# Moving the products with v and the pool differences in a fused decoder layer

## The chip, the cores and the metric

One core of a Trainium2 chip runs the whole layer in one launch. The engines used are TensorE (PE, with its weight loads PEld), VectorE (DVE), ScalarE (ACT), GpSimd (POOL) and the DMA queues that SyncE (SP), GpSimd and ScalarE fill. The metric is device time of one execution in microseconds (us), the median of the runs shown.

## What is computed

The layer takes x (512 tokens by 1024 channels, float32). One projection gives q, k, v, the input p of a pool branch and the gate logits g. The part that matters here is this, cut from the reference:

```python
q, k, v, p, g = jnp.split(proj, [ATTN_WIDTH, 2 * ATTN_WIDTH, 3 * ATTN_WIDTH, 3 * ATTN_WIDTH + POOL_WIDTH], axis=-1)
y_attn = moba_attention(q.reshape(hs), k.reshape(hs), v.reshape(hs), rel_bias) @ w_branch_attn[l]
y_pool = multiscale_pool(p, w_pool_group[l], pool_scale[l]) @ w_branch_pool[l]
...
for g, w in enumerate((2, 4, 8, 16)):                  # in multiscale_pool: 4 groups of 128 channels
    outs.append((csg[:, 1:] - lag) / cnt[None, :, None])   # mean over the last w tokens
diff = pooled - p
y = jnp.einsum('bsgc,gcd->bsgd', diff, w_group) * scale
```

Attention has 8 heads of 64 channels with a causal mask and a bias by distance. Both branches are projected, weighted by sigmoid gates, summed, projected again and normalised; a gated MLP with a causal convolution follows.

## The kernel before

Nearly every product is split: an operand a is rounded to a_hi (ACT, line 69) and the rest a_lo = a - a_hi is taken on DVE (line 70), and three matmuls hi*hi, lo*hi, hi*lo are summed in PSUM (`mm3`, lines 213, 216 and 217). Weights come in tiles of 128 x 1024 through a ring: load into `wraw`, then split into `whi` and `wlo`. `weights(i)` calls `fetch()` so that three tiles beyond the one in use have been requested (`LEAD`). The products with v (line 575) are plain float32 with a stationary operand of 64 columns, one head writing the lower and the other the upper 64 partitions of one PSUM bank.

A part of the tiles is computed in pairs with seven products in place of eight (`seven`, line 246). Each pair uses four weight tiles: A (plain), X (two loads, the second accumulating: SP at line 164, then POOL at line 165), D (SP, line 160) and Y (formed on DVE at line 175 from X and A). The matmuls of a pair write the banks named `sai`, `sbi` and `sci`. The last product of a pair, `close`, is deferred and runs when the next pair calls `flush()`. Line 267 is the final add of a pair but for that deferred product; it is kept as `state["add"]`.

In time, the part around the change runs like this. First come x and v, then pool groups 3 and 2 as plain tiles (`in_tile("p", ...)`, `PLAIN = (3, 2)`). Then the loop over n runs five pairs: n = 0 gives pool groups 0 and 1, n = 1 to 4 give two heads each (q and k tiles). Then a loop over the eight heads h does for each head: `head(h + 2)` prepares q and k, one gate tile (`in_tile`, 24 matmuls named `g`), `scores(h + 2)`, the transposes of the probabilities (`trans(h)`, line 562, copied to `PT` by ACT at 564 and DVE at 565 and 566), and for odd h `pv(h // 2)`, the products with v of both heads of a pair (16 matmuls, line 575, bank `ob`). `PT` has two buffers.

A pool group has three steps. `pool_sum` copies the projection into a padded tile and adds shifted copies (line 427), log2(w) times: four for group 3 (on DVE), three for group 2, one for group 0 and two for group 1 (on POOL). `pool_dif` forms mean minus token (lines 438 to 440, tile `dif`) and splits it into `difs`. `pool_out` makes three matmuls into bank `zb` and copies to `zT`. The tiles of sums and differences share a ring of four buffers, tag `tmp`; `difs` has two.

The order on each engine is fixed when the kernel is built. A scheduler takes the instructions traced in program order, earlier ones first where several are ready by its own model of time, and lays down one sequence for each engine and DMA queue; on the chip an instruction that waits holds everything behind it in its own sequence. `tc.issue_after(ins)` adds a constraint: what the block traces on the engine of `ins` stands behind `ins` in that engine's sequence. `AHEAD` says how many fetches early a raw tile of a pair is requested.

Of the kernel before, what the change touches and what calls it, by code (L numbers as in the profile page):

```python
# [8 lines left out]
F32 = mybir.dt.float32  # L9
F32R = mybir.dt.float32r  # L10
AF = mybir.ActivationFunctionType
ALU = mybir.AluOpType
PSUM = bass.MemoryType.PSUM

P = 128
S = 512
# [3 lines left out]
H = 8  # L20
# [10 lines left out]
PAD = 16  # L31
LEAD = 3
RING = 5
TMP = 4
PLAIN = (3, 2)
# [10 lines left out]
def layer_kernel(ctx: ExitStack, tc: tile.TileContext, xT, x, w_v, w_c, rel_bias, invcnt, w_group,  # L46
                 pscale, w_br, w_out, lnr, w_fi, convp, w_fo, out):
    nc = tc.nc
# [16 lines left out]
    def split(hi, lo, src, copy=None):  # L65
        if copy:
            copy(hi, src)
        else:
            nc.scalar.activation(hi, src, AF.Copy)  # L69
        state["lo"] = nc.vector.tensor_tensor(lo, src, hi.bitcast(F32), op=ALU.subtract)  # L70
        return state["lo"]
# [42 lines left out]
    state = {"next": 0, "limit": WO0 - 1}  # L114

    def fetch(pool=None, early=None):
        i = state["next"]
        state["next"] = i + 1
        for q, ahead in AHEAD.items():
            while coming[q]:  # L120
                key = coming[q][0]
                n, f = key
                if not homes.get((n, q)) or at[n, f, q] > i + (ahead if q != "A" or (n, f - 1) in pair_of else 0):
                    break
                fetch_raw(coming[q].pop(0), q)
        if isinstance(chunks[i], tuple):
            ready[i] = (fetch_fo if i >= FO0 else fetch_seven)(i, *chunks[i])
            return
        raw = wp.tile([P, D], F32, tag="wraw", name=f"wraw{i}", bufs=3)
        if pool is None:  # L130
            hi = wp.tile([P, D], F32R, tag="whi", name=f"whi{i}", bufs=RING)
            lo = wp.tile([P, D], F32R, tag="wlo", name=f"wlo{i}", bufs=RING)
        else:
            hi = pool.tile([P, D], F32R, name=f"whi{i}")
            lo = pool.tile([P, D], F32R, name=f"wlo{i}")
        parts = 2 if early else 1
        for c in range(parts):
            sl = slice(c * (D // parts), (c + 1) * (D // parts))
            (nc.scalar if early else nc.sync).dma_start(raw[:, sl], chunks[i][:, sl])
            split(hi[:, sl], lo[:, sl], raw[:, sl], fast if early and c == 0 else None)  # L140
            if c == 0 and early:
                early()
        ready[i] = (hi, lo)
# [10 lines left out]
    def fetch_raw(key, q):  # L154
        a, u = pair_of[key]
        r = raws[key, q] = homes[key[0], q](key[1])
        if q == "A":
            nc.sync.dma_start(r, a)
        elif q == "D":
            nc.sync.dma_start(r, u[:, S:])  # L160
        else:
            v = r.rearrange("p (a c) -> p a c", a=2)
            (pst, pn), (est, _) = u.ap
            nc.sync.dma_start(v, bass.AP(tensor=u.tensor, offset=u.offset, ap=[[pst, pn], [0, 2], [est, S]]))
            state["acc"] = nc.gpsimd.dma_start(  # L165
                v, bass.AP(tensor=a.tensor, offset=a.offset, ap=[[pst, pn], [u.offset + S - a.offset, 2], [est, S]]),
                accum_op=ALU.add)
# [58 lines left out]
    def flush():  # L226
        if pending:
            pending.pop()()
# [63 lines left out]
    pb = pooling.enter_context(tc.tile_pool(name="pb", bufs=1, side="right", reuse_waits="tile"))  # L292
# [35 lines left out]
    cinv = const.tile([P, PAD], F32, name="cinv")  # L328
# [61 lines left out]
    dif = {}  # L390
# [26 lines left out]
    def pool_sum(j, b, sign=1.0, eng=None):  # L417
        eng = eng or nc.gpsimd
        w = POOL_WINDOWS[j]
        pt = pb.tile([P, PAD + S], F32, tag="tmp", name=f"pt{j}", bufs=TMP)  # L420
        nc.gpsimd.memset(pt[:, :PAD], 0.0)
        nc.scalar.activation(pt[:, PAD:], b, AF.Copy, scale=sign)
        cur, sh = pt, 1
        while sh < w:
            nxt = pb.tile([P, PAD + S], F32, tag="tmp", name=f"pw{j}_{sh}", bufs=TMP)
            o = 2 * sh - 1
            eng.tensor_tensor(nxt[:, o:], cur[:, o:], cur[:, o - sh:PAD + S - sh], op=ALU.add)
            cur, sh = nxt, 2 * sh
        sums[j] = pt, cur

    def pool_dif(j, *behind):
        w = POOL_WINDOWS[j]
        pt, cur = sums.pop(j)
        with ExitStack() as held:
            for ins in behind:
                held.enter_context(tc.issue_after(ins.ins))
            d = pb.tile([P, S], F32, tag="tmp", name=f"dif{j}", bufs=TMP)
            nc.vector.scalar_tensor_tensor(d, cur[:, PAD:], 1.0 / w, pt[:, PAD:], op0=ALU.mult, op1=ALU.subtract)
            nc.vector.tensor_tensor(d[:, :w - 1], cur[:, PAD:PAD + w - 1], cinv[:, :w - 1], op=ALU.mult)
            nc.vector.tensor_tensor(d[:, :w - 1], d[:, :w - 1], pt[:, PAD:PAD + w - 1], op=ALU.subtract)  # L440
            dd = pb.tile([P, 2, S], F32R, tag="dif", name=f"difs{j}", bufs=2)
            dif[j] = dd[:, 0, :], dd[:, 1, :]
            split(*dif[j], d)

    def pool_out(j):
        b = bank(f"zb{j}")
        mm3(b, (wg_hi[:, j, :], wg_lo[:, j, :]), dif[j], True, True)
        nc.scalar.activation(zT[:, j, :], b, AF.Copy, scale=psc[:, j:j + 1])

    def in_tile(kind, j):  # L450
        wh, wl = split3(weights(at[kind, j]), KT)
        b = bank(f"{kind}{j}")
        for kt in range(KT):
            mm3(b, (wh[:, kt, :], wl[:, kt, :]), (xT_hi[:, kt, :], xT_lo[:, kt, :]), kt == 0, kt == KT - 1)
        if kind == "p":
            pool_sum(j, b, eng=nc.vector if j == PLAIN[0] else None)
        else:
            gslot[j] = gates[:, len(gslot), :]
            nc.vector.tensor_copy(gslot[j], b)
# [9 lines left out]
    raw_q = {}  # L469
    raw_k = {}  # L470
    in_tile("p", PLAIN[0])
    pool_dif(PLAIN[0])
    in_tile("p", PLAIN[1])

# [40 lines left out]
    for n in range(1 + pairs):  # L515
        if n == 0:
            u, done = xr[1][:, 3, :], lambda ba, u: pool_sum(0, ba)
        else:
            u = raw_k[n - 1] = av.tile([P, S], F32, tag="rk", name=f"rk{n - 1}")
            done = lambda ba, u, p=n - 1: heads_done(p, ba)  # L520
        seven(("i", n), (xT_hi, xT_lo), ti, xr[1][:, 2, n % 2 * 256:n % 2 * 256 + 256], u, done)
        if n == 0:
            pool_dif(PLAIN[1], state["add"])
            with tc.issue_after(state["acc"].ins):
                write_table(*table)
        elif n == 1:
            pool_dif(0, state["add"])
            pool_sum(1, xr[1][:, 3, :], -1.0)
            for j in PLAIN:
                pool_out(j)  # L530
        elif n == 2:
            pool_dif(1, state["add"])
            with tc.issue_after(state["acc"].ins):
                load_strip(0)
                load_strip(1)
            head(0, state["add"], state["copy"])
        elif n == 3:
            pool_out(0)
            pool_out(1)
            head(1, state["add"], state["copy"])  # L540
            pooling.close()
            aw = attn.enter_context(tc.tile_pool(name="aw", bufs=3, side="right", reuse_waits="tile"))
            scores(0)
# [25 lines left out]
    def pv(p):  # L569
        b = bank(f"ob{p}")  # L570
        for kb in range(NT):
            n = (NT - kb) * P
            for e in range(2):
                h = 2 * p + e
                nc.tensor.matmul(b[e * DH:(e + 1) * DH, kb * P:], vv[:, kb, h * DH:(h + 1) * DH],
                                 PTs[h][:, toff[kb]:toff[kb] + n], start=kb == 0, stop=kb == NT - 1)
        state["o"] = nc.scalar.activation(oT[:, p, :], b, AF.Copy)

    scores(1)
    for h in range(H):  # L580
        if h + 2 < H:
            head(h + 2, nms[h], exps[h])
        if h < H - 1:
            in_tile(*fill.pop(0))
            flush()
        if h + 2 < H:
            scores(h + 2)
        trans(h)
        if h >= 4:
            with tc.issue_after(nms[h].ins), tc.issue_after(exps[h].ins):  # L590
                split(zT_hi[:, h - 4, :], zT_lo[:, h - 4, :], zT[:, h - 4, :])
        if h == H - 1:
            in_tile(*fill.pop(0))
        if h % 2:
            pv(h // 2)
    attn.close()

    bra = ExitStack()
# [74 lines left out]
    for f in range(GSEVEN, KT):  # L673
        if f == KT - 1:
# [3 lines left out]
              lambda ba, u, f=f: gate_done(f, ba, u), first_half if f == KT - 1 else None)  # L678
# [214 lines left out]
    for f in range(last + 1, NF):  # L893
# [24 lines left out]
        for c in list(spread):  # L918
            if f >= KH + c.stop - 1 and (f > last + 1):
# [3 lines left out]
                                               op0=ALU.mult, op1=ALU.subtract)  # L923
# [167 lines left out]
```

## Time and profile before

| | before |
|---|---|
| median of 3 runs | 652.54 us (651.95 to 653.64) |
| the profiled execution | 653.2 us, of which span 651.5 us |
| instructions | 10192 |
| granted TensorE clock, mean | 0.993 |
| PE between 50 and 62 us | 8.11 us busy of 12.00 |
| PE between 66 and 80 us | 14.00 us busy of 14.00 |

Busy time is time in which an engine works on an instruction. Matmuls are pipelined, so a row's duration is longer than the step from one matmul to the next. In a row of an engine's sequence the columns are start, duration, engine, line, operation and operands; a bracket at the end gives the idle time before it and what ended it. A row of the waits is: who waited, for whom, then us in total, times and the longest.

### The profile page before, as it was taken

The page shows a single profiled execution, that of the slowest core. Times are in us where ns is not written, and L with a number is a line of the kernel's source. Part 1 is how long each engine was busy: PE and PEld are TensorE (multiplying, and loading weights), DVE is VectorE, ACT ScalarE, POOL GpSimd, SP SyncE. Part 2 cuts the span into 40 slices and gives each one's busy share as a digit, 9 for nine tenths or more (in the row PEclk, how much of TensorE's full clock was granted, in tenths as well). Part 3 has the DMA queues.
Part 4 walks back from the last instruction along what each step waited for, and adds up shares of the span by engine and source line. Part 5 has one row for each costly group of instructions (what it writes and reads, how often), then busy time and mean ns, then how long its engine had stood idle before and what let it go on. Part 6 is the DMA issues. An engine that isn't in the chain of part 4 may idle for free.

```text
span 651.5 us, 10192 instructions
## 1 busy us (share of the span) xinstructions
PE 633.7 (97%) x3910; PEld 562.6 (86%) x3910; DVE 497.3 (76%) x754; ACT 348.9 (54%) x522; POOL 115.4 (18%) x131
## 2 busy tenths in 40 slices
PE   9987999999999999999999999999999999999994
PEld 6877998777688999888998999999998888888884
DVE  6967788667477597759795788888889649798695
ACT  6634667554472555605364466566556337555452
POOL 0033305322115111210001010110101201123202
PEclk9999999999999999999999999999999999999998
DMA  8676627432158544553147767777727964889905
GB/s 315 205 165 157 160 69 244 131 97 58 58 173 213 151 111 136 177 205 103 60 149 190 174 168 194 179 196 192 179 68 274 266 201 100 207 191 198 273 1 129
DMA packets 39328, 106.11 MB, mean 163 GB/s; under 512 B 4320, under 2 KB 4584, under 8 KB 39024
## 3 DMA queue, kind: packets, MB, share of 16 engines
q1 hardware_dynamic: 26560, 71.37, 33.5%
q0 software_dynamic: 12144, 33.06, 26.0%
q10 hardware_dynamic: 576, 1.05, 0.4%
q8 instruction: 30, 0.49, 0.3%
q14 instruction: 18, 0.15, 0.1%
HBM read 100.20 MB, written 3.17 MB: 159 GB/s over the span
## 4 chain that ended last, share of the span: by engine, by line
PE 93%; DVE 3%; issue 1%; ACT 1%; POOL 1%; DMA 0%; DVEq 0%; POOLq 0%; ACTq 0%
PE fi L213 5%; PE fi L216 5%; PE fi L217 5%; PE saf L213 4%; PE saf L217 4%; PE saf L216 4%; PE v L387 3%; PE g L213 2%; PE br L213 2%; PE g L217 2%; PE wo L217 2%; PE br L216 2%; PE br L217 2%; PE wo L216 2%; PE wo L213 2%; PE g L216 2%
## 5 line engine op out<-in xcount | busy, mean ns | idle before, releaser
L70 DVE TENSOR_TENSOR wlo<-wraw,whi 128x1024 fp32r<-128x1024 f32 (+1 forms) x59 | 71.9, 1226 | 17.1 <-ACT whi L69 16.9
L69 ACT ACTIVATE whi<-wraw 128x1024 fp32r<-128x1024 f32 (+1 forms) x58 | 59.5, 1034 | 44.5 <-DMA wraw<-in_w_fo 9.7
L70 DVE TENSOR_TENSOR wlo<-araw,whi 128x1024 fp32r<-128x1024 f32 x46 | 55.9, 1221 | 9.2 <-ACT whi L69 8.4
L69 ACT ACTIVATE whi<-araw 128x1024 fp32r<-128x1024 f32 x46 | 48.1, 1058 | 20.9 <-PE saf L216 6.1
L216 PE MATMUL fi<-hT_lo,whi 128*128 128x512 f32 (+1 forms) x168 | 56.7, 339 | 0.0
L217 PE MATMUL fi<-hT_hi,wlo 128*128 128x512 f32 (+1 forms) x168 | 56.7, 339 | 0.0
L213 PE MATMUL fi<-hT_hi,whi 128*128 128x512 f32 (+1 forms) x168 | 56.4, 340 | 0.0
L165 POOL DMA_DIRECT2D xraw<-in_w_fi x14 | 16.9, 1210 | 161.8 <-DVE y L831 51.5
L69 ACT ACTIVATE whi<-tw 128x1024 fp32r<-128x1024 f32 (+1 forms) x30 | 29.4, 982 | 21.9 <-PE fi L216 8.7
L70 DVE TENSOR_TENSOR wlo<-tw,whi 128x1024 fp32r<-128x1024 f32 (+1 forms) x30 | 33.3, 1125 | 6.8 <-ACT whi L69 6.7
L217 PEld LDWEIGHTS fi<-hT_hi,wlo 128*128 128x128 f32 x168 | 31.9, 190 | 3.5
L216 PEld LDWEIGHTS fi<-hT_lo,whi 128*128 128x128 f32 x168 | 31.9, 190 | 3.3
L213 PEld LDWEIGHTS fi<-hT_hi,whi 128*128 128x128 f32 x168 | 31.6, 190 | 3.4
L216 PE MATMUL saf<-hT_lo,whi 128*128 128x256 f32 x112 | 31.6, 282 | 0.0
L213 PE MATMUL saf<-hT_hi,whi 128*128 128x256 f32 x112 | 31.6, 282 | 0.0
L217 PE MATMUL saf<-hT_hi,wlo 128*128 128x256 f32 x112 | 31.5, 282 | 0.0
L213 PE MATMUL sbf<-T_hi,whi 128*128 128x256 f32 x112 | 31.3, 280 | 0.0
L213 PE MATMUL saf<-nT_hi,whi 128*128 128x256 f32 x112 | 31.3, 279 | 0.0
L217 PE MATMUL saf<-nT_hi,wlo 128*128 128x256 f32 x112 | 31.3, 279 | 0.0
L217 PE MATMUL sbf<-T_hi,wlo 128*128 128x256 f32 x112 | 31.2, 279 | 0.0
L216 PE MATMUL saf<-nT_lo,whi 128*128 128x256 f32 x112 | 31.2, 279 | 0.0
L216 PE MATMUL sbf<-T_lo,whi 128*128 128x256 f32 x112 | 31.2, 279 | 0.0
(347 smaller groups left out, 2110.2 us busy)
## 6 DMA issues: line engine op xcount, KB each, us to landing
tw<-in_w_fo POOLq DMA_DIRECT2D x20, 512.0 KB, 7.9
wraw<-in_w_fi SPq DMA_DIRECT2D x16, 512.0 KB, 3.7
araw<-in_w_fi SPq DMA_DIRECT2D x14, 512.0 KB, 3.9
xraw<-in_w_fi SPq DMA_DIRECT2D x14, 512.0 KB, 4.8
xraw<-in_w_fi POOLq DMA_DIRECT2D x14, 512.0 KB, 7.2
wraw<-in_w_c SPq DMA_DIRECT2D x10, 512.0 KB, 4.2
tw<-in_w_fo SPq DMA_DIRECT2D x10, 512.0 KB, 7.0
wraw<-in_w_fo SPq DMA_DIRECT2D x10, 512.0 KB, 9.1
```

What stands on the lines that cost most here:

```text
L69: nc.scalar.activation(hi, src, AF.Copy)
L70: state["lo"] = nc.vector.tensor_tensor(lo, src, hi.bitcast(F32), op=ALU.subtract)
L165: state["acc"] = nc.gpsimd.dma_start(v, bass.AP(tensor=a.tensor, offset=a.offset, ap=[[pst, pn], [u.offset + S - a.offset, 2], [est, S]]), ...
L213: ins = nc.tensor.matmul(out_, wh, ah, start=start, stop=False, **kw)
L216: nc.tensor.matmul(out_, wh, al, start=False, stop=False, **kw)
L217: nc.tensor.matmul(out_, wl, ah, start=False, stop=stop, **kw)
L387: nc.tensor.matmul(bs[j], xs_[j][a], (wh, wl)[b], start=kt == 0 and n == 0, stop=False)
```

## The change

Six edits. X of pair n = 1 is requested three fetches ahead, not five. The last sum of a group is kept as `state["sum"]`. The difference is formed in place, in the buffer of the last sum, the edge columns first. From the difference of group 3 up to the end of pair n = 0, DVE work is constrained behind group 3's last sum. The product of group 3 keeps its pair but is traced first there; the difference of group 2 moves from n = 0 to n = 1 and its product from n = 1 to n = 2; the difference of group 1, in n = 2, is constrained behind the final add of n = 1 and no longer that of n = 2. In the loop over heads, `pv` of a pair is traced one head later, behind the next gate tile and ahead of `scores` and `trans`; the last pair's stays at the end.

```diff
@@ fetch
                 n, f = key
+                if (n, f, q) == ("i", 1, "X"):
+                    ahead = 3
                 if not homes.get((n, q)) or at[n, f, q] > i + (ahead if q != "A" or (n, f - 1) in pair_of else 0):
@@ pool_sum
-            eng.tensor_tensor(nxt[:, o:], cur[:, o:], cur[:, o - sh:PAD + S - sh], op=ALU.add)
+            state["sum"] = eng.tensor_tensor(nxt[:, o:], cur[:, o:], cur[:, o - sh:PAD + S - sh], op=ALU.add)
@@ pool_dif
-            d = pb.tile([P, S], F32, tag="tmp", name=f"dif{j}", bufs=TMP)
-            nc.vector.scalar_tensor_tensor(d, cur[:, PAD:], 1.0 / w, pt[:, PAD:], op0=ALU.mult, op1=ALU.subtract)
-            nc.vector.tensor_tensor(d[:, :w - 1], cur[:, PAD:PAD + w - 1], cinv[:, :w - 1], op=ALU.mult)
-            nc.vector.tensor_tensor(d[:, :w - 1], d[:, :w - 1], pt[:, PAD:PAD + w - 1], op=ALU.subtract)
+            d, x_ = cur[:, PAD:], pt[:, PAD:]
+            nc.vector.tensor_tensor(d[:, :w - 1], d[:, :w - 1], cinv[:, :w - 1], op=ALU.mult)
+            nc.vector.scalar_tensor_tensor(d[:, w - 1:], d[:, w - 1:], 1.0 / w, x_[:, w - 1:], op0=ALU.mult,
+                                           op1=ALU.subtract)
+            nc.vector.tensor_tensor(d[:, :w - 1], d[:, :w - 1], x_[:, :w - 1], op=ALU.subtract)
@@ behind the first plain tile
 in_tile("p", PLAIN[0])
+    behind_sum = ExitStack()
+    behind_sum.enter_context(tc.issue_after(state["sum"].ins))
     pool_dif(PLAIN[0])
     in_tile("p", PLAIN[1])
@@ loop over pairs
         if n == 0:
-            pool_dif(PLAIN[1], state["add"])
+            behind_sum.close()
             with tc.issue_after(state["acc"].ins):
                 write_table(*table)
         elif n == 1:
+            pool_out(PLAIN[0])
+            pool_dif(PLAIN[1], state["add"])
             pool_dif(0, state["add"])
             pool_sum(1, xr[1][:, 3, :], -1.0)
-            for j in PLAIN:
-                pool_out(j)
+            add1 = state["add"]
         elif n == 2:
-            pool_dif(1, state["add"])
+            pool_out(PLAIN[1])
+            pool_dif(1, add1)
@@ loop over heads
             in_tile(*fill.pop(0))
             flush()
+        if h and h % 2 == 0:
+            pv(h // 2 - 1)
         if h + 2 < H:
             scores(h + 2)
         trans(h)
@@
             in_tile(*fill.pop(0))
-        if h % 2:
-            pv(h // 2)
+    pv(H // 2 - 1)
     attn.close()
```

## The prediction

> **What bounds the kernel now.** I read the page, then the waits of PE, then stretches of the span, then the places where PE stops, row by row.
>
> ```profile
> PE 633.7 (97%) x3910; PEld 562.6 (86%) x3910; DVE 497.3 (76%) x754; ACT 348.9 (54%) x522; POOL 115.4 (18%) x131
> ```
> ```profile
> PE zb L213 <- ACT difs L69: 4.5, 2, 4.0
> PE sai L213 <- DVE sai L267: 1.0, 1, 1.0
> ```
> ```profile
> 40.00:50.00 10.00, 8.22 (x63) 7.38 (x62) 9.55 (x14) 4.99 (x9) 2.85 (x5) 1.00 0.67 167
> 120.00:140.00 20.00, 20.00 (x102) 14.96 (x101) 13.21 (x34) 11.12 (x26) 6.18 (x10) 1.00 0.41 107
> ```
>
> The columns of a stretch are its length, then busy time of PE, weight loads, DVE, ACT, POOL, then granted clock and DMA. PE is the bound: 97% of the span, and all of 120 to 140, where DMA is busy 0.41. So PE time saved early should reach the end, since nothing else is full and the weight loads are released by the same work. The largest wait of PE is on the split difference of a pool group, 4.00 us in one piece:
>
> ```profile
> 62.11 0.50 PE L213 MATMUL zb<-difs,wg_hi 128*128 128x512 f32 x1 [4.00 <-ACT difs L69]
> ```
> ```profile
> 46.37 1.20 POOL L165 DMA_DIRECT2D xr<-in_w_c  x1 [11.07 <-DVE pw L427]
> 49.55 1.06 POOL L427 TENSOR_TENSOR pw<-pt 128x527 f32<-128x527 f32 x1 [0.78 <-DVE dif L439]
> 50.69 1.39 POOL L427 TENSOR_TENSOR pw<-pw 128x525 f32<-128x525 f32 x1
> 55.49 1.27 POOL L165 DMA_DIRECT2D xr<-in_w_c  x1 [3.41 <-DMA xr<-in_w_c]
> 56.32 1.54 POOL L427 TENSOR_TENSOR pw<-pw 128x521 f32<-128x521 f32 x1
> ```
> ```profile
> 57.89 0.69 DVE L438 SCALAR_TENSOR_TENSOR dif<-pw,pt 128x512 f32<-128x512 f32 x1 [3.34 <-POOL pw L427]
> 58.50 1.22 DVE L70 TENSOR_TENSOR wlo<-araw,whi 128x1024 fp32r<-128x1024 f32 x1
> 61.42 0.63 ACT L69 ACTIVATE difs<-dif 128x512 fp32r<-128x512 f32 x1 [2.94 <-DVE dif L440]
> ```
> ```profile
> L440 DVE TENSOR_TENSOR dif<-dif,pt x4: 156/168/1027, 49.4 to 83.2; 128x15 f32<-128x15 f32 x1, 128x7 f32<-128x7 f32 x1, 128x1 f32<-128x1 f32 x1, 128x3 f32<-128x3 f32 x1
> ```
>
> Three sums on POOL mark group 2, window 8. Its third on POOL waits behind a DMA issue that itself waits for a load; DVE waits for that sum, with the weight split of the next pair behind it (58.50); ACT waits for DVE; PE for ACT. The stop also slows what follows:
>
> ```profile
> 62.40:65.90 3.50, 3.50 (x18) 3.45 (x18) 2.26 (x4) 0.83 (x2) 0.00 (x0) 0.52 0.41 132
> 66.00:69.50 3.50, 3.50 (x29) 3.42 (x29) 1.98 (x4) 2.14 (x4) 1.76 (x3) 1.00 0.29 93
> ```
>
> In the 3.5 us after it the granted clock is 0.52 and 18 matmuls pass, later 29 in the same time. Eighteen at the later pace take 18 x 3.50 / 29 = 2.2 us, so the low clock costs 1.3 us. The stop is worth 4.0 + 1.3 = **5.3 us**.
>
> **Part 1: group 2's difference and product one pair later.** Three DVE operations, the split (ACT, DVE), three matmuls and the ACT copy into zT go behind the final add of pair 1. They issue no DMA and are the same work; the products' PE time moves with them. At the stop PE then goes on with the next pair's matmuls. These need the split that stood behind the waiting difference at 58.50; DVE had been idle 3.34 us before 57.89, so it moves up into that gap. I take the whole stop as gone: -5.3 us. The bounds are -5.3 and 0 (the product is put again where its operand is late). What is late next is pair 2's sequence of splits, and the moved group, whose DVE work now falls here:
>
> ```profile
> 67.94 0.43 DVE L267 TENSOR_TENSOR sai<-xr,sci 128x256 f32<-128x256 f32 x1
> 66.00:80.00 14.00, 14.00 (x118) 13.92 (x118) 11.57 (x17) 9.77 (x15) 6.20 (x7) 1.00 0.64 164
> ```
>
> The moved operations cost 0.69 for the difference, 0.17 each (median above) for its two corrections at the edge and 0.68 for the split (the row at 63.05 below), 1.7 us of DVE, in 14 us of which DVE has 2.4 free. It fits, barely, and DVE enters the stretch earlier than before. Group 1's difference goes the other way, behind the add of pair 1 and no longer that of pair 2. That feeds the other stop on a pool product:
>
> ```profile
> 85.73 0.50 PE L213 MATMUL zb<-difs,wg_hi 128*128 128x512 f32 x1 [0.51 <-ACT difs L69]
> ```
>
> It should vanish: -0.5, bounds -0.5 and +0.5 (as late again). The wait of 1.0 at L267 later on I leave as it is.
>
> **Part 2: the four sums of group 3 first on DVE, the difference in place, X of pair 1 later.**
>
> ```profile
> 38.59 0.69 DVE L175 TENSOR_TENSOR araw<-xr,araw 128x512 f32<-128x512 f32 x1 [7.01 <-DMA xr<-in_w_c]
> 40.42 1.22 DVE L70 TENSOR_TENSOR wlo<-xr,whi 128x1024 fp32r<-128x1024 f32 x1
> 42.78 1.22 DVE L70 TENSOR_TENSOR wlo<-araw,whi 128x1024 fp32r<-128x1024 f32 x1
> 45.66 0.68 DVE L427 TENSOR_TENSOR pw<-pw 128x513 f32<-128x513 f32 x1
> ```
> ```profile
> L69 ACT ACTIVATE whi<-araw 128x1024 fp32r<-128x1024 f32 x46 | 48.1, 1058 | 20.9 <-PE saf L216 6.1
> ```
>
> Before, the sums stand behind an addition that waits 7.01 us for pair 0's X. With the new order they can run in that gap: four of 0.68 make 2.7 us, part of which stood ahead of the Y split at 42.78. The gain is at most PE's idle time here: PE is busy 8.22 of 10 us from 40 to 50, so 1.8 us. Against it: additions and the D and Y splits must now follow all four sums, and the split of X (40.42), traced ahead of the scope, may still stand between two sums and hold the rest until X has landed. Then Y is late: split of X from 39.7 (38.59 and 1.06 of rounding on ACT) to 40.9, two sums 1.4, the difference 0.7, two additions 1.4, rounding 1.06, split 1.22: 46.7, where it ended at 44.0; so +2.7. Which order the scheduler's plan takes cannot be seen; I take 0, between -1.8 and +2.7. The in-place difference is three instructions of the same sizes, one buffer of four fewer: the copy of group 2 into the ring comes sooner, and no operation waits more. Cost 0.
>
> ```profile
> 25.55 0.90 SPq L164 DMA_DIRECT2D xr<-in_w_c  x2
> 30.18 0.82 SPq L160 DMA_DIRECT2D xr<-in_w_c  x2
> ```
> ```profile
> 32.66 2.64 POOL L165 DMA_DIRECT2D xr<-in_w_c  x2 [31.11 <-DMA xr<-in_w_c]
> 51.57 0.28 PE L213 MATMUL sbi<-iT_hi,whi 128*128 128x256 f32 x1
> xr<-in_w_c POOLq DMA_DIRECT2D x4, 512.0 KB, 6.9
> ```
>
> X of pair 1 is two transfers, on SP and then accumulating on POOL. Traced later, both can move past the two D loads on SP (30.18) and past the sums of group 2 on POOL. Pair 0's X then has the engines to itself and lands sooner. PE uses pair 1's X at 51.57; landing 6.9, rounding 1.06 and split 1.22 before that put its last harmless issue on POOL at 42.4, against 32.66 now. Cost 0 with 9 us of cover; each microsecond beyond 42.4 is one of PE.
>
> **Part 3: products with v one gate tile later.**
>
> ```profile
> 119.20 1.00 PE ob L575 x2
> 120.20 0.43 PE g L213
> 120.63 0.23 PE g L216
> ...
> 124.30 1.00 PE ob L575 x3
> ...
> 127.36 1.44 PE ob L575 x8
> ...
> 176.00 2.30 PE ob L575 x16
> ```
>
> Sixteen matmuls belong to a pair of heads (the chain counts only those that are not covered by a neighbour). Pair 0 has them in three runs, 1.00 + 1.00 + 1.44 = 3.44 us, pair 3 (heads alternating) in one of 2.30; the two heads write different halves of the partitions and overlap when adjacent. The matmul after each run takes 0.43 and not 0.23, so two fewer runs save 0.4. One run for each of three pairs gives 3 x 1.54 = -4.6; pair 3 is as it was. The other end is 0 (the plan cuts as before). Where the plan believed the odd head's operands ready shows in the order:
>
> ```profile
> 127.08 0.28 PE L497 MATMUL sc<-kl,q 128*128 128x256 f32 x1
> 127.29 1.51 PE L575 MATMUL ob<-PT,vv 128*64 128x384 f32 x10
> ```
>
> In pair 0 the last ten came after score matmuls that follow the gate tile, so a cut behind the first six may stay; I take it for pair 1 too. Six are one overlapped run of 1.00 and one even-head matmul pair of 384 columns alone, 0.75 (1.00 x 384/512): 1.75 + 1.44 = 3.19, with one run fewer 0.45 saved. Two pairs so, one whole: **-2.4 us**. Moved past 24 gate matmuls, the run delays only the ACT copy to oT (read after the loop) and the release of two PT buffers, still ahead of the next transposes.
>
> **Sum.** -5.3 - 0.5 + 0 - 2.4 = -8.2. The profiled run took 653.2 us (span 651.5), so 645.0; it lies 0.7 above the median, 652.54, which gives **644.3**.
>
> **Rivals.**
> A, first pair late on DVE: the X split stays between the sums, and group 2's sums, now sooner, run on POOL beside DVE.
>
> ```profile
> 51.42 1.22 DVE L70 TENSOR_TENSOR wlo<-xr,whi 128x512 fp32r<-128x512 f32 x1
> 63.05 0.68 DVE L70 TENSOR_TENSOR difs<-dif,difs 128x512 fp32r<-128x512 f32 x1
> ```
>
> A split of 512 takes 0.68 alone and 1.22 beside the POOL sum of 50.69: +0.54, three times 1.6. With +2.7 that is +4.3: 648.6. For it: DVE is busy 9.55 of 10 us there. Against: the 7.01 us gap ahead. Chance 15%. [...]
>
> B, the products with v are cut at the same places: 646.7 (12%). For it: the plan's order above; against: the odd head's copies have a whole gate tile more.
>
> C, the stop on a pool product only moves: PE meets group 2's product before its split, behind the add at 67.94 and the weight splits between; 5.3 back, 649.6 (8%). Against: a whole pair's matmuls stand ahead.
>
> D, slower: X of pair 1 is issued on POOL behind the three sums of group 2. If those start where POOL was free in the run of before, behind the issue at 46.37, they end at 47.6 + 4.0 = 51.6; landing, rounding and split end at 60.8, PE idles 9.2 and pays 1.3 for the clock: +10.5, 654.8. An issue at 49.3 breaks even. Against: the copy comes sooner. Chance 8%.
>
> **Numbers.** Forecast 57%, by itself from 640.3 (products at 4.6, Part 2 at its gain) to 647.0 (Part 2 at its loss). The range 639.5 to 651 holds A, B, C; D lies outside. A measurement tells 0.3%, 2 us, from no change. Faster 0.83; same 0.09 (A and C at their worst, D in part); slower 0.08 (D).
>
> **What would show it.** PE's waits without a 4 us row at zb, granted clock 1.00 from 58 to 70; ob rows of x16 (or x6 and x10) with about 2.3 to 3.2 us a pair; sums ahead of the araw additions on DVE. Wrong: a wait of PE at sbi or sai beyond 2 us in the first two pairs, POOL's second L165 issue behind L427, or a zb wait at a new place.

## The result and the profile after

| | before | after |
|---|---|---|
| median | 652.79 us (651.95 to 653.64, 4 runs) | 648.23 us (647.59 to 648.72, 4 runs) |
| the profiled execution | 653.2 us, span 651.5 | 648.35 us, span 646.6 |

The ratio is 0.9929, interval 0.9912 to 0.9947: 4.6 us faster, where the forecast was 8.2 us faster (644.3); the time lies inside the stated range of 639.5 to 651. In the lines of after, line numbers above 120 stand two to eight higher than in before: the split products are at 215, 218 and 219, the sums at 429, the additions for Y at 177, the transposes at 570, the products with v at 583.

The page of after, busy time of the engines:

```profile
PE 630.8 (98%) x3910; PEld 563.1 (87%) x3910; DVE 497.2 (77%) x754; ACT 349.0 (54%) x522; POOL 120.1 (19%) x131
```

The waits of PE in after (who waited, for whom, us in total, times, longest):

```profile
PE sai L215 <- ACT whi L69: 4.3, 2, 4.2
PE warm_ps L310 <- DVE warm L307: 1.2, 1, 1.2
PE tr L570 <- DVE nm L506: 0.8, 1, 0.8
PE v L389 <- DVE whi L279: 0.5, 1, 0.5
```

The row at `zb` is gone, and with it the 1.0 at `sai` behind line 267 and the 1.0 at `sbi`. In their place PE waits 4.2 us in one piece for a rounded weight, in the first pair. The stretches (length, PE, weight loads, DVE, ACT, POOL, clock, DMA) show both sides:

```profile
40.00:50.00 10.00, 5.66 (x33) 5.16 (x32) 8.93 (x13) 4.61 (x7) 4.05 (x5) 0.77 0.39 125
50.00:62.00 12.00, 12.00 (x92) 11.81 (x92) 9.49 (x12) 5.84 (x9) 3.50 (x6) 0.91 0.71 151
62.00:66.00 4.00, 4.00 (x36) 4.00 (x35) 1.61 (x3) 1.40 (x3) 1.43 (x1) 1.00 0.88 279
```

From 50 to 66 PE is now full, where it idled 4 us. From 40 to 50 it is busy 5.66 us and no longer 8.22, at a clock of 0.77. Row by row, PE in after:

```profile
41.80 0.28 PE L219 MATMUL sbi<-iT_hi,wlo 128*128 128x256 f32 x1
46.27 0.58 PE L215 MATMUL sai<-inT_hi,whi 128*128 128x256 f32 x1 [4.19 <-ACT whi L69]
...
49.08 0.42 PE L215 MATMUL sai<-inT_hi,whi 128*128 128x256 f32 x1
49.30 0.42 PE L218 MATMUL sai<-inT_lo,whi 128*128 128x256 f32 x1
...
52.07 0.34 PE L215 MATMUL sai<-xT_hi,whi 128*128 128x256 f32 x1
52.25 0.28 PE L218 MATMUL sai<-xT_lo,whi 128*128 128x256 f32 x1
```

Behind the stop a matmul of 256 columns lasts 0.41 and not 0.28, and the next follows after 0.213 (fifteen steps from 47.59 to 50.79) and not 0.118 (from 52.25 on). That goes on from 46.27 to 52.07, with a granted clock of 0.50. At these steps 5.8 us hold 3.2 us of work at the full pace, so the low clock costs **2.6 us** on top of the 4.2. The weight that PE waits for is Y's. DVE, which forms it, in after:

```profile
33.83 0.71 DVE L429 TENSOR_TENSOR pw<-pw 128x525 f32<-128x525 f32 x1
39.21 1.23 DVE L70 TENSOR_TENSOR wlo<-xr,whi 128x1024 fp32r<-128x1024 f32 x1 [4.68 <-ACT whi L69]
40.36 1.42 DVE L429 TENSOR_TENSOR pw<-pw 128x521 f32<-128x521 f32 x2
41.70 0.69 DVE L70 TENSOR_TENSOR wlo<-xr,whi 128x512 fp32r<-128x512 f32 x1
42.30 1.55 DVE L177 TENSOR_TENSOR araw<-xr,araw 128x512 f32<-128x512 f32 x1
...
44.45 0.68 DVE L177 TENSOR_TENSOR araw<-araw 128x512 f32<-128x512 f32 x1
...
49.15 2.70 DVE L70 TENSOR_TENSOR wlo<-xr,whi 128x1024 fp32r<-128x1024 f32 x1
```

Two sums, then X's split, for which DVE stands 4.68 us, then the other two sums, and only then the additions that make Y. ACT in after rounds X first, then Y:

```profile
38.12 1.58 ACT L69 ACTIVATE whi<-xr 128x1024 fp32r<-128x1024 f32 x2 [5.14 <-DMA xr<-in_w_c]
...
45.16 2.00 ACT L69 ACTIVATE whi<-araw 128x1024 fp32r<-128x1024 f32 x2 [3.14 <-DVE araw L177]
```

The first of the two roundings of Y ends at 46.2, and PE starts at 46.27. POOL in after:

```profile
31.68 2.64 POOL L167 DMA_DIRECT2D xr<-in_w_c  x2 [30.13 <-DMA xr<-in_w_c]
...
41.95 1.35 POOL L429 TENSOR_TENSOR pw<-pt 128x527 f32<-128x527 f32 x1 [0.73 <-DVE pw L429]
...
49.24 1.52 POOL L429 TENSOR_TENSOR pw<-pw 128x521 f32<-128x521 f32 x1
```

Pair 1's X is still issued with pair 0's (x2 at 31.68). The sums of group 2 start at 41.95, where before had the first at 49.55, and the DVE operations beside them take 1.55 for 0.68 (42.30) and 2.70 for 1.22 (49.15).

The products with v, from the chain of waits of after (start, us, engine, operation, count):

```profile
122.69 1.65 PE ob L583 x6
...
124.89 1.44 PE ob L583 x8
...
141.88 1.65 PE ob L583 x6
...
144.20 1.44 PE ob L583 x8
...
161.06 2.31 PE ob L583 x16
...
171.18 2.30 PE ob L583 x16
```

### The profile page after: what moved, and what is told of

Same layout as the page of the kernel before. It is cut to its first block, busy times and chain, and to the rows that moved or that the text cites. A ratio compares the mean times of both kernels' runs of the same rounds, so it can differ in the third digit from the quotient of the medians.

```text
span 646.6 us, 10196 instructions
## 1 busy us (share of the span) xinstructions
PE 630.8 (98%) x3910; PEld 563.1 (87%) x3910; DVE 497.2 (77%) x754; ACT 349.0 (54%) x522; POOL 120.1 (19%) x131
## 4 chain that ended last, share of the span: by engine, by line
PE 91%; DMA 4%; DVE 3%; issue 1%; ACT 0%; DVEq 0%; SPq 0%; POOLq 0%; ACTq 0%
PE fi L215 5%; PE fi L218 5%; PE fi L219 5%; PE saf L215 4%; PE saf L219 4%; PE saf L218 4%; PE g L215 2%; PE br L215 2%; PE g L218 2%; PE g L219 2%; PE br L219 2%; PE wo L218 2%; PE br L218 2%; PE wo L219 2%; PE wo L215 2%; PE sbf L215 2%
## 5 line engine op out<-in xcount | busy, mean ns | idle before, releaser
L517 POOL TENSOR_SCALAR pp<-pp,rs 128x128 f32<-128x128 f32 (+3 forms) x32 | 26.6, 846 | 29.9 <-DVE rs L514 29.9
```

Source lines behind the costliest of these rows:

```text
L517: nc.gpsimd.tensor_scalar(pp[:, offs[i]:offs[i] + n], pp[:, offs[i]:offs[i] + n], rs[:, i:i + 1], 1.0, op0=ALU.mult, op1=ALU.mult)
```

## Experiments

Theory: the pool moves give what Part 1 says and the products with v what Part 3 says. The rest is taken back by the constraint that holds DVE work behind group 3's last sum: X's split stands between the sums, so Y is late, PE stops, and the clock falls. Rivals: the products with v give nothing, or the DVE time lost beside POOL makes the stop. e1 to e4 ran beside before on one chip (before 651.88 us), e5 to e8 on another (652.15); so kernels of different chips are compared by their ratios.

**e1: the constraint taken out**, all else as in after.

```diff
     behind_sum = ExitStack()
-    behind_sum.enter_context(tc.issue_after(state["sum"].ins))
     pool_dif(PLAIN[0])
```

> The changed kernel without the constraint that puts DVE work of group 2 and pair 0 behind group 3's last sum. Theory (the constraint puts the two additions that form pair 0's Y behind four sums, two of which stand behind the split of X, so that PE stops 4.2 us and then runs 5.9 us at half clock): the 4.2 us wait of PE at sai goes, waits of about 1 to 2 us in all at the weight splits of the first pair come back, and the time falls by 4 to 6 us to about 643. Rival (the additions are late because POOL's sums of group 2 now run beside DVE, whatever the order): a wait of 3 us or more stays at sai and the time stays within 1 us of 648.2.

Measured: 644.1 us, ratio 0.9863 (0.983 to 0.9895), against 0.9929 for after: the constraint costs 0.0066 of 652, 4.3 us (the two intervals leave 2 to 7). The profiled execution, 647.05 us, was the slowest of the four. The 4.2 us wait for Y is gone. PE now waits 1.9 us at the same matmul, for something else; ACT in e1:

```profile
39.61 1.58 ACT L69 ACTIVATE whi<-xr 128x1024 fp32r<-128x1024 f32 x2 [4.37 <-DMA xr<-in_w_c]
41.56 2.01 ACT L69 ACTIVATE whi<-araw 128x1024 fp32r<-128x1024 f32 x2 [0.37 <-DVE araw L177]
45.66 0.60 ACT L424 ACTIVATE pt<-p 128x512 f32<-128x512 f32 x1 [2.09 <-DVE pw L429]
46.15 0.38 ACT L256 ACTIVATE xr<-sai 128x256 f32<-128x256 f32 x1
```

From the start of X's rounding to the start of Y's pass 1.95 us here (39.61 to 41.56) and 7.04 in after (38.12 to 45.16). By the rows of DVE, the 5.1 us between them are the wait for X's rounding and X's split (2.2), one sum more (0.7), the split of D at 41.70 (0.6), the difference (0.7) and the time lost beside POOL at 42.30 (0.9). So the rival of the POOL sums, which e1 moves too (the first to 49.58), makes about a sixth of it, and the order of DVE the rest.

The copy of group 2 into its padded tile waits until a sum on DVE has released one of the four buffers, and the copy that releases the bank `sai` (line 256) stands behind it in ACT's sequence. By these rows that is the next bound. No run shows it: none has a fifth buffer, which might lift it.

**e2: after without the move of the products with v; e3: that move alone, on before.**

```diff
# e2, from after
-        if h and h % 2 == 0:
-            pv(h // 2 - 1)
...
-    pv(H // 2 - 1)
+        if h % 2:
+            pv(h // 2)
# e3, from before: the same lines the other way round
```

> The changed kernel with the products with v queued as before. Theory (the products with v save 2.6 us, from 3.44 to 3.09, 3.09 and 2.31 us of PE in three pairs and 0.2 us for each of four runs saved, independent of the rest): about 650.8, 2.0 us below the kernel before. Rival (the products with v give nothing, and the whole gain is the pool part's): 648.2.

> The kernel before with only the products with v one gate tile later. Theory: runs of 6 and 10, 6 and 10, 16 on PE, about 650.2 (2.6 us less than before), and the 4.0 us wait at zb unchanged. Rival (moved products give nothing, as the pair's overlap is only in the records): 652.8.

Measured: e2 650.1 us, ratio 0.9969 (0.9952 to 0.9986); e3 648.95 us, ratio 0.9959 (0.9935 to 0.9982). The move is worth 0.0041 in e3 and 0.9969 - 0.9929 = 0.0040 in after, 2.6 to 2.7 us both times (1 to 4 by the intervals). The chain of waits of e3 shows it cut like after's:

```profile
125.99 1.65 PE ob L575 x6
...
128.31 1.44 PE ob L575 x8
...
145.19 1.65 PE ob L575 x6
...
147.38 1.44 PE ob L575 x8
...
164.37 2.31 PE ob L575 x16
```

The waits of e3 and then of e2 show that each half leaves the other's place alone; e3 keeps before's stop at `zb`, e2 has after's at `sai`:

```profile
PE zb L213 <- ACT difs L69: 5.6, 2, 5.1
```
```profile
PE sai L215 <- ACT whi L69: 2.8, 2, 2.4
```

The stop of e2 was 2.4 us long in its profiled execution, and no low clock followed it (1.00 in every stretch up to 80 us); that execution, 648.22 us, was the quickest of its ten. Its mean granted clock was 0.997, that of the other nine 0.990 to 0.994, which suggests that the low clock came in some of those. The profiled execution of e3, 652.25 us, was the slowest of its ten. So a stop and a low clock in one profile are those of one execution.

**e4: the products with v behind the scores** of the next head, still ahead of its transposes.

```diff
-        if h and h % 2 == 0:
-            pv(h // 2 - 1)
         if h + 2 < H:
             scores(h + 2)
+        if h and h % 2 == 0:
+            pv(h // 2 - 1)
         trans(h)
```

> The changed kernel with the products with v behind the scores of the same round, ahead of the transposes. Theory (what is left is the cut behind six matmuls in pairs 0 and 1, since the plan holds the odd head's second block for late): one run of sixteen in 2.3 us in each pair, 0.8 us of PE and one run less in two pairs, 2.0 us in all: about 646.2. Rival (the transposes' copies wait for the products and give it back): 648.2 or more, with a wait at the transposes or the next products.

Measured: 646.27 us, ratio 0.9907 (0.988 to 0.9934). The chain of e4 has sixteen in one run for every pair:

```profile
123.52 2.30 PE ob L583 x16
...
141.67 2.30 PE ob L583 x16
...
158.53 2.31 PE ob L583 x16
```

Against after's 1.65 + 1.44 = 3.09 that is 0.8 us in each of two pairs, 1.6 us, and 0.9929 - 0.9907 makes 1.4 us. The two intervals overlap, so it is the rows and not the ratio that show it.

**e5: the constraint kept, X's split moved behind all four sums.** No tile from pair 0's X on is requested until group 3's tile and its sums are traced.

```diff
+    state["limit"] = at["i", 0, "X"] - 1
     in_tile("p", PLAIN[0])
+    state["limit"] = WO0 - 1
     behind_sum = ExitStack()
```

> The changed kernel with the fetch of pair 0's X traced one tile later, so that its split on DVE too stands behind group 3's four sums, which then run in DVE's idle time before X lands. [...] Rival (the sums' place is of no weight, X lands too late for anything): wait and time as in the changed kernel, 648.2.

Measured: 645.31 us, ratio 0.9895 (0.9866 to 0.9924). DVE in e5:

```profile
33.18 0.71 DVE L429 TENSOR_TENSOR pw<-pt 128x527 f32<-128x527 f32 x1 [1.92 <-ACT pt L424]
33.93 2.17 DVE L429 TENSOR_TENSOR pw<-pw 128x525 f32<-128x525 f32 x3
37.80 2.72 DVE L70 TENSOR_TENSOR wlo<-xr,whi 128x1024 fp32r<-128x1024 f32 x2 [1.70 <-ACT whi L69]
40.45 0.68 DVE L177 TENSOR_TENSOR araw<-xr,araw 128x512 f32<-128x512 f32 x1
```

All four sums now stand in the gap ahead of X, and the first addition for Y at 40.45 and not 42.30. PE in e5:

```profile
43.54 0.39 PE L215 MATMUL sai<-inT_hi,whi 128*128 128x256 f32 x1 [1.37 <-ACT whi L69]
...
44.49 0.39 PE L215 MATMUL sai<-xT_hi,whi 128*128 128x256 f32 x1 [0.45 <-ACT whi L69]
...
45.19 0.28 PE L215 MATMUL sai<-inT_hi,whi 128*128 128x256 f32 x1
...
45.67 0.42 PE L215 MATMUL sai<-inT_hi,whi 128*128 128x256 f32 x1
```

The stop is 1.37 + 0.45 us, 2.5 less than after's 4.19 + 0.15. Where X's split stood explains only a part. From the start of X's rounding to that of Y's pass 5.72 us (36.71 to 42.43) and not 7.04, so the order makes 1.3 of the 5.1 us of the constraint. The rest of the shorter stop is that X landed earlier in this execution: its rounding began 5.5 us before PE's stop and not 4.0. In e2 and e4, whose order on DVE is after's up to Y, the same distance is 7.04 us again, and the first stops were 2.40 and 3.48 us. Yet in e5 the clock halves (0.83 in the stretch from 40 to 50 us), 0.9 us after the second piece of the stop has ended. The ratios put the gain over after at 0.0034, 2.2 us, the two spans at 3.3; the two intervals overlap, so that e5 is faster than after at all is likely, not shown.

**e7: the pool moves alone, with the difference in place** (e1 without the move of the products with v), and **e6: both, without the constraint and with the products behind the scores** (the diffs of e1 and e4 together).

```diff
# both, from after
-    behind_sum.enter_context(tc.issue_after(state["sum"].ins))
...
# e7
-        if h and h % 2 == 0:
-            pv(h // 2 - 1)
...
-    pv(H // 2 - 1)
+        if h % 2:
+            pv(h // 2)
# e6
-        if h and h % 2 == 0:
-            pv(h // 2 - 1)
         if h + 2 < H:
             scores(h + 2)
+        if h and h % 2 == 0:
+            pv(h // 2 - 1)
```

> The changed kernel without the constraint and with the products with v as before: the move of the pool differences and products by a pair is what is left (with the difference in place). Theory (the stop at zb is worth 5.3 us and the small one 0.5, and all of it comes back once nothing delays the first pair): 5 to 6 us below the kernel before, 0.8 to 0.9%, with no wait at zb. Rival (part of the stop was covered, or moves into the first pairs): less than 0.5% below.

> The changed kernel without the constraint behind group 3's last sum and with the products with v behind the scores: both edits that gained by themselves. Theory (they act at different places on PE, so they add): about 2 us below the kernel without the constraint alone, 1.7% below the kernel before. Rival (the wait that the one takes away comes back later in the other): no faster than 1.4% below.

Measured: e7 646.06 us, ratio 0.9899 (0.9877 to 0.9921); e6 **641.45 us**, ratio 0.9828 (0.9804 to 0.9852), the fastest of all, and 0.0101 or 6.6 us below after. The waits of e7 and then of e6 have one row of PE left in the pairs:

```profile
PE sai L215 <- ACT xr L256: 1.6, 1, 1.6
```
```profile
PE sai L215 <- ACT xr L256: 1.5, 1, 1.5
```

No row shows a low clock in either (1.00 in every stretch from 24 to 80 us). With e3 the parts add up: 0.0101 + 0.0041 = 0.0142, and e1, which has both, shows 0.0137.

**e8: e6 with the sums of group 2 on DVE too**, so that no POOL sum of groups 3 and 2 runs beside DVE.

```diff
-            pool_sum(j, b, eng=nc.vector if j == PLAIN[0] else None)
+            pool_sum(j, b, eng=nc.vector if j in PLAIN else None)
```

> The kernel of the run with both edits, with group 2's three sums on DVE too, none of them on POOL. [...] Rival (DVE is the bound there and three more instructions cost what they take): slower by about 2 us, with a wait at the weight splits or sai.

Measured: 642.65 us, ratio 0.9845 (0.9811 to 0.9879); not to be told from e6. A stop of 1.75 us was followed by the low clock in its profile (0.83 in the stretch from 40 to 50 us). DVE time is lost beside POOL (0.87 and 1.48 us in after, at 42.30 and 49.15), but paying for the sums on DVE is no better.

## Why the prediction was right in direction and half right in size

**The sum, by the profiles.** Stops of PE at `sbi`, `sai` and `zb` are the rows of the waits, each of one execution; the low clock is the time of the slow matmuls times 0.447, from the steps of 0.213 and 0.118 us.

| us | stops in the pairs | low clock | sum |
|---|---|---|---|
| before | 7.1 (4.5 + 1.0 + 1.0 + 0.6) | 1.4 (62.58 to 65.79) | 8.5 |
| after | 4.3 | 2.6 (46.27 to 52.07) | 6.9 |
| e7, no constraint | 1.6 | 0 | 1.6 |

From before to e7 that is 6.9 us, less the wait of 0.8 at `tr` that is new in e7, so 6.1; the spans differ by 651.5 - 643.9 = 7.6, and these rows do not show where the other 1.5 went. From e7 to after the constraint adds 5.3, and the spans rise by 2.7, so the products with v take off 2.6.

**Part 1 was right** in its mechanism: 5.3 + 0.5 were taken, and e7 measured 6.1 us (652.15 - 646.06), 6.6 by the ratio (5.2 to 8.0). No run has the moves without the difference in place. The stop at 62.11 and the one at 85.73 are gone and did not come back at a new `zb`, so rival C fell. The wait of 1.0 at `sai` behind line 267, which the prediction left as it was, went too, and so did the 1.0 at `sbi`. A wait of 0.8 at `tr` is new; it is there in every kernel with the pool moves.

**Part 2 is the step that failed.** It was taken at 0 between -1.8 and +2.7, with the sums in the gap ahead of X's split or around it left open. The order that came was rival A's, X's split between the second and third sum, in the place that rival A gave it: Y's first rounding was put at 45.5 (46.7 less the split of 1.22) and ended at 46.2. The stop grew from 1.0 + 0.6 to 4.3 us, +2.7, the far end of the bound. That it fits so well is in part luck: with the same order e2 and e4 stopped for 2.8 and 3.9 us in all, as X landed earlier or later. What no end of the bound held is the clock: 2.6 us lost at half clock behind that stop. The prediction had charged the stop at `zb` for its clock, and rival D too, but not rival A. So Part 2 measured 2.7 + 2.6 = +5.3 us in the profiles, and e1 beside after +4.3 us in the ratios. The measured time stayed in the range only because the range held this rival; the sum itself, 644.3, was 3.9 off. Rival A's result, 648.6, lies 0.4 from the measured 648.23, but partly by luck: it put 1.6 us on three POOL sums beside DVE. They cost DVE 0.87 (42.30) and 1.48 us (49.15) in two places, of which only the first lies ahead of the stop. Rival A at its worst, and with it the upper end of the range, 651, is shown by no run.

The addition of 42.30 and the split of 49.15 end 0.55 and 1.09 us after the POOL sums beside them have ended (43.30 and 50.76), nearly their usual 0.68 and 1.22; the split's row starts 0.09 us before the POOL sum's. It is not so at every meeting in after: the POOL sum of 73.19 took 3.35 us, where that of 49.55 in before took 1.06, and the DVE rows of 512 columns that began inside it (73.72, 74.33 and 74.93) took their usual 0.68. No run shows what decides which of the two takes longer.

On POOL the first two sums of group 2 now stand ahead of pair 2's X (the issue of 48.47), which before came ahead of them (46.37). Pair 1's X stays where it was, and the sequences laid down with three fetches ahead and with five are the same on every engine, so that edit does nothing and rival D had no ground. That the in-place difference lets the copy of group 2 come sooner was right, but by one sum only: without the constraint (e1) the copy starts at 45.66, behind the third sum of group 3, where before had it at 46.38, behind the fourth, and the first sum of group 2 starts no sooner (49.58 and 49.55). The 41.95 of after comes with the constraint, which lets two sums of group 3 run ahead of X. The copy also holds ACT, as e1 shows, where the prediction had said that no operation waits more.

**Part 3 was right**, cut included: 6 + 10, 6 + 10, and 16 in one run, as taken. Rival B fell. It was forecast at 2.4 us; e3 and e2 give 2.6 to 2.7. A run of six took 1.65 (1.75 taken). The whole gain that was named as the other end is there once the scores stand ahead (e4, e6): the odd head's last ten matmuls are then no longer placed behind them.

With Part 2 at +4.3 the sum is -5.3 - 0.5 + 4.3 - 2.4 = -3.9; measured -4.6.

## What to carry over

A constraint that holds an engine's later work behind one operation also holds it behind whatever the scheduler has put ahead of that operation; look up what waits there before adding it (here X's split, for which DVE stood 4.68 us). Price every new stop of TensorE twice, for its length and for the half clock that may follow (4.2 and 2.6 us in after; none followed in the profiles of e2, e6 and e7). Of an edit that has several aims, run each alone: here one line took back 4.3 us of the 8.9 that the others gave (e1).

## What was not expected of the hardware

In these profiles the half clock lasted one length or twice that. Read from the granted clock in steps of 0.05 us, it lasted 3.41 us in before (from 62.54), e1 (47.05), e3 (63.22), e4 (48.00), e5 (45.37) and e8 (45.28), and 6.83 us in after (45.35 to 52.18). In after it began while PE still stood, 0.9 us before the first matmul; in e8 it began 1.1 us after PE was back (44.18), with full speed between. The length of the stop does not decide: it came behind stops of 1.37 + 0.45 us (e5), 1.75 (e8) and 1.87 (e1), and not behind 2.40 + 0.45 (e2), 1.63 (e7) and 1.51 (e6). The clock by the stretch from 40 to 50 us, of e5 and then of e2:

```profile
40.00:50.00 10.00, 8.19 (x53) 7.68 (x52) 8.93 (x12) 4.50 (x7) 4.50 (x6) 0.83 0.62 170
```
```profile
40.00:50.00 10.00, 7.16 (x57) 6.70 (x56) 8.93 (x12) 5.03 (x9) 5.63 (x8) 1.00 0.44 138
```

More idle time, and yet no loss of clock in e2. What PE did in the 3.41 us ahead of the fall does not decide either. It was busy for 0.43 us of them in before, 0.13 in after, 1.54 in e1, 0.00 in e3, 1.12 in e4, 1.60 in e5 and 1.66 in e8. Where the clock did not fall, the stretch of that length around the stop holds 1.90 in e6 and 1.78 in e7, more than any of these, but 0.56 in e2. So why the clock falls behind one stop and not behind another is not shown by these ten profiles.
